# Tap sums of a depthwise convolution kept in PSUM, and two gate blocks ordered behind the last mLSTM head, in a fused RWKV-7, convolution and mLSTM block

## The chip, the core and the metric

One core of a Trainium2 chip runs the whole block as one program. The metric is the device time of one execution in microseconds (us), as the median of several runs. TensorE (PE) multiplies, VectorE (DVE) and ScalarE (ACT) do elementwise work, GpSimd (POOL) does elementwise work beside them, and SyncE's queue (SP) issues all DMAs of this kernel.

## The reference, cut to what matters

```python
def _conv_branch(u, dw, db, ln_w, ln_b, rows):
    a, g = jnp.split(u, 2, axis=-1)
    z = a * jax.nn.sigmoid(g)
    z = _depthwise_conv(z.reshape(B * rows, GRID_W, CONV_W), dw, db)   # 31 taps in rows of 64
    return jax.nn.silu(_layernorm(z, ln_w, ln_b, LN_EPS))
...
def _merge(u_gate, ya, yb, yc, pa, pb, pc, wo):
    ga, gb, gc = jnp.split(jax.nn.sigmoid(u_gate), N_BRANCH, axis=-1)
    m = ga * (ya @ pa) + gb * (yb @ pb) + gc * (yc @ pc)
    return m @ wo
...
# reference(): 512 latent tokens, 256 context tokens, width 1024
h = _rmsnorm(x, g_norm1) * (1 + mod_x[1]) + mod_x[0]
u_rw, u_cv, u_ml, u_gate = jnp.split(h @ w_in, ...)
ya = _rwkv_mixer(...)      # 8 heads, two directions
yc = _mlstm_mixer(...)     # 4 heads of width 128, two directions
yb = _conv_branch(u_cv, ...)                       # 512 channels
x = x + mod_x[2] * _merge(u_gate, ya, yb, yc, ...)
x = x + mod_x[5] * _mlp(h2, w_mlp1, w_mlp2)
return _rmsnorm(x, g_final)
```

`u_gate` is 3072 columns wide: 24 blocks of 128, of which the stage looked at here computes the first six. The convolution's 512 channels are four tiles of 128 channels by 512 tokens.

## The kernel before, in words

Every product with a weight is made in three: a 128x512 half block of weights (`raw`) is loaded by SP, ACT casts it to its high part (`whi`, line 159), POOL subtracts that from `raw` (`wlo`, line 160), and PE multiplies high by high, high by low and low by high (line 293 in this stage). `raw` has three buffers, `whi` and `wlo` four each, so a `wlo` that is late holds back the next load, and the load is a place in SP's queue on which everything behind it waits. `dense(b)` loads block `b` (`wload`) and makes its 24 products of 128x512 for the 512 latent tokens (tile `dl`), and 24 of 128x256 for the context where asked (`dc`). Its PSUM tiles rotate through two banks.

The order of the work: norms and modulation; the features of the RWKV heads, with the first two convolution tiles; the **mLSTM stage** (about 260 to 530 us of the span), with the last two convolution tiles; four pairs of RWKV heads as a recurrent chain (`weave`), with the other 18 gate blocks and the projections beside it; merge and MLP.

In the mLSTM stage `front(h)` makes the four dense blocks of head `h` (`kT`, `vT`, `qT`, `to`), transposes `kT` and `vT`, and builds the states of five chunks for each direction: POOL scales a chunk of keys (`kw`, line 836), PE multiplies it with the values into a PSUM tile `st` (two buffers, line 838), DVE adds it to the running state (`Cst`, lines 840 and 842). `back(h)` makes the scores (`psc`, line 850), the decay masks (`gbc`, `Wd`), per chunk the products `acc` (lines 872 and 873), their normalisation on DVE (lines 875 to 888), four transposes (`pt`, line 889), the gated result `yc` and its store. Traced in this order: `front(0)`, `front(1)`, `back(0)`, the taps of convolution tiles 2 and 3, the preparation of the first RWKV pair (`rw.ctx(0)`, `rw.lat(0)`), `front(2)`, `back(1)`, `front(3)`, `back(2)`, `back(3)`, and six gate blocks `dense(B_GA + g)`, each with a tanh on ACT (line 524) and a store (line 525).

`taps` (line 317) runs over 31 taps of two tiles in turn. Each of its instructions on DVE takes the input tile `z` shifted by one more token, times a weight per channel, plus the sum `y`, into `y` (line 324). Before the change `z` and `y` both lie in SBUF.

Each engine runs its instructions strictly in the order in which the program was built. That order is made by the framework's planner when the program is built: it follows a simulated timeline with costs of its own, takes what is traced first where several instructions are ready, and otherwise fills in later work that is ready. So the taps, the dense blocks and the gate blocks are spread among other work by that plan, not by the chip. `tc.issue_after(ins)` adds to each instruction traced in its block, on the engine of `ins`, that it stands behind `ins` in that engine's order. It makes no semaphore.

Pools share memory as stacks. The RWKV pools opened after the stage lie over what it leaves: the chain's `UV` tiles over the `whi` and `wlo` buffers, its `SV` tiles over `cols`, `kT`, `vT` and the first `qT` buffer, its `xc` and `sps` over both `qT` buffers. The gate results use the tag `qT`. PSUM has eight banks: in this stage two for dense tiles, two for `tp`/`st`, two for `sc` (`psc`, `acc`, `pt`), and on the right side two for the RWKV pool `psa` (tags `g` and `m`).

Of the kernel before, what the change touches and what calls it, by code (L numbers as in the profile page):

```python
# [7 lines left out]
F32 = mybir.dt.float32  # L8
# [6 lines left out]
PSUM = bass.MemoryType.PSUM  # L15
DRAM = bass.MemoryType.DRAM

P = 128
D = 1024
NT = 512  # L20
# [21 lines left out]
B_RW, B_CV, B_ML, B_MG, B_GA = 0, 15, 23, 39, 40  # L42
# [14 lines left out]
NGA = 6  # L57
# [19 lines left out]
def build(tc, wblk, wada, xin, cin, params, lora, consts, rowp, out, dbg=None):  # L77
    nc = tc.nc
    V, A, G, PE, SY = nc.vector, nc.scalar, nc.gpsimd, nc.tensor, nc.sync
# [18 lines left out]
    def CN(name):  # L98
        return cst[:, CO[name]:CO[name] + 128]

    ident = CN("ident")
# [27 lines left out]
    sp = {}  # L129
# [24 lines left out]
    def whalf(b, x, W=None, nr=NRAW, nh=NHI):  # L154
        raw = (W or W0).tile([P, 512], F32, tag="raw", name="raw", bufs=nr)
        SY.dma_start(raw[:, :], wblk[b, :, x * 512:x * 512 + 512])
        hi = (W or W0).tile([P, 512], F32R, tag="hi", name="whi", bufs=nh)
        lo = (W or W0).tile([P, 512], F32R, tag="lo", name="wlo", bufs=nh)
        A.copy(hi[:, :], raw[:, :])  # L159
        G.tensor_tensor(lo[:, :], raw[:, :], hi[:, :], ALU.subtract)  # L160
        return hi, lo

    def wload(b, W=None):
        return [whalf(b, x, W) for x in range(2)]
# [32 lines left out]
    for i in range(4):  # L197
        t = S0.tile([P, D], F32, name=f"xt{i}")
# [3 lines left out]
    for q in range(8):  # L202
        t = S0.tile([P, 4, 512], F32, tag="wada", name="wada", bufs=8)
        SY.dma_start(t[:, :, :], wada[q].rearrange("p (k m) -> p k m", k=4))
        wa.append(t)
        if q == 3:
            for i in range(2):
                t = S0.tile([P, D], F32, name=f"ct{i}")
# [35 lines left out]
    for q in range(4):  # L244
# [5 lines left out]
        pt = PS0.tile([P, 4, 2], F32, tag="pm", name="pm", bufs=1)  # L250
# [27 lines left out]

    PS1 = ed.enter_context(tc.tile_pool(name="ps1", bufs=1, space=PSUM, reuse_waits="tile"))

    def dense(b, lat=True, ctx=False, M=P):
        wts = wload(b)
        res = []
        for seg, use in enumerate((lat, ctx)):
            if not use:
                continue
            ps_ = PSD.tile([P, (NT, NC_)[seg]], F32, tag="d", name=("dl", "dc")[seg], bufs=ND)
            n = 0
            for k in range(KT):
                hi, lo = wts[k // 4]  # L290
                ko = k % 4 * P
                for w, x in ((hi, hh), (hi, hl), (lo, hh)):
                    PE.matmul(ps_[0:M, :], lhsT=w[:, ko:ko + M], rhs=x[seg][:, k, :],  # L293
                              start=(n == 0), stop=(n == 3 * KT - 1))
                    n += 1
            res.append(ps_)
        return res
# [28 lines left out]
    tiles = []  # L326
    for i in range(2):
        z, y = SO.tile([P, 752], F32, name=f"z{i}"), SO.tile([P, NT], F32, name=f"cy{i}")
# [6 lines left out]
    def shifted(b, ctx, name, bufs=1, dst=None):  # L335

        pss = dense(B_RW + b, True, ctx)
        if dst is None:
            dst = S1.tile([P, T if ctx else NT], F32, tag=name, name=name, bufs=bufs)[:, :]
        for ps, a, z in zip(pss, (0, NT), (NT, T)):  # L340
            n = z - a
            A.activation(dst[:, a:z], ps[:, :], AF.Copy, scale=om[:, b:b + 1])
            V.scalar_tensor_tensor(dst[:, a + 1:z], ps[:, 0:n - 1], C("mu_p", b), dst[:, a + 1:z], ALU.mult, ALU.add)
            V.scalar_tensor_tensor(dst[:, a:z - 1], ps[:, 1:n], C("mu_n", b), dst[:, a:z - 1], ALU.mult, ALU.add)
        return dst
# [63 lines left out]
    t = shifted(12, True, "vj", 2)  # L409
    A.activation(wdt[:, :], t, AF.Tanh)  # L410
    t = shifted(13, True, "vj", 2)
# [62 lines left out]
    t = shifted(14, False, "vj", 2)  # L474
# [22 lines left out]
    ec = ExitStack()  # L497
    CZ = ec.enter_context(tc.tile_pool(name="cz", bufs=1, side="right", reuse_waits="tile"))
    SG = eg.enter_context(tc.tile_pool(name="mlg", bufs=1, side="right", reuse_waits="tile"))
    front, back = mlstm(tc, nc, SM, SG, PS1, dense, CN, C, ident, nwh, epsc, sp, sp_rows, dump, consts)  # L500
    eg.close()
    st = [None] * 4
    tiles = [(i, CZ.tile([P, 752], F32, name=f"cz{i}")[:, :], CZ.tile([P, NT], F32, name=f"cy{i}")[:, :]) for i in (2, 3)]
    for i, z, y in tiles:
        SY.dma_start(z, sp["z", i][:, :])
    st[0] = front(0)
# [1 line left out]
    back(0, *st[0])  # L508
    taps(tiles)
    for i, z, y in tiles:  # L510
        SY.dma_start(sp["yb", i][:, :], y)
    ec.close()
    rw = Rwkv(tc, CN, C, ident, epsc, PL, sp, dump)
    rw.open_a()
# [2 lines left out]
    back(1, *st[1])  # L517
    st[3] = front(3)
    back(2, *st[2])
    back(3, *st[3])  # L520
    for g in range(NGA):
        ps, = dense(B_GA + g)
        t = SM.tile([P, NT], F32, tag="qT", name="gt", bufs=2)
        A.activation(t[:, :], ps[:, :], AF.Tanh, scale=0.5)
        SY.dma_start(sp["g", g][:, :], t[:, :])
# [27 lines left out]
    acc = {}  # L553
# [165 lines left out]
def mlstm(tc, nc, S, SG, PS1, dense, CN, C, ident, nwh, epsc, sp, sp_rows, dump, consts):  # L719
    V, A, G, PE, SY = nc.vector, nc.scalar, nc.gpsimd, nc.tensor, nc.sync  # L720
# [21 lines left out]
    b = SG.tile([R, T], F32, name="b")  # L742
# [8 lines left out]
    g = t1.rearrange("p (c t) -> p c t", c=6)  # L751
# [27 lines left out]
    for c2 in range(2):  # L779
        pt = PS1.tile([P, 3, 3, R], F32, tag="tp", name="tp", bufs=2)  # L780
        for ci in range(3):
            c = c2 * 3 + ci
# [64 lines left out]
    def back(h, qT, kT, to, v1, qs, Cst):  # L847
        psc = PS1.tile([P, NT], F32, tag="sc", name="psc", bufs=2)
        for c in range(4):
            PE.matmul(psc[:, c * 128:(c + 1) * 128], lhsT=kT[:, c * 128:(c + 1) * 128], rhs=qT[:, c * 128:(c + 1) * 128],  # L850
                      start=True, stop=True)
        Wd = []
        for d in range(2):
            rr = rows[d] + h
            gbc = S.tile([P, NT], F32, tag="gbc", name="gbc", bufs=2)
            SY.dma_start(gbc[:, :], sp_rows[d][h:h + 1, 0:NT].partition_broadcast(P))
            nm = nms[:, d * 128:d * 128 + 128]
            for c in range(4):
                V.scalar_tensor_tensor(gbc[:, c * 128:(c + 1) * 128], gbc[:, c * 128:(c + 1) * 128],
                                       cols[:, c, 0, rr:rr + 1], nm, ALU.add, ALU.add)  # L860
            A.activation(gbc[:, :], gbc[:, :], AF.Exp)
            wd = S.tile([P, NT], F32, tag="Wd", name="Wd", bufs=2)
            V.tensor_tensor(wd[:, :], psc[:, :], gbc[:, :], ALU.mult)
            Wd.append(wd)
        ht = S.tile([P, 4, 128], F32, tag="ht", name="ht")
        stats = S.tile([P, 4, 6], F32, tag="stats", name="stats")
        mv = S.tile([P, 4, 2], F32, tag="mv", name="mv")
        for c in range(4):
            acc = PS1.tile([P, 2, 129], F32, tag="sc", name="acc", bufs=2)
            for d in range(2):  # L870
                p = orders[d].index(c)
                PE.matmul(acc[:, d, :], lhsT=Wd[d][:, c * 128:(c + 1) * 128], rhs=v1[:, c, :], start=True, stop=False)
                PE.matmul(acc[:, d, :], lhsT=qs[d][:, c * 128:(c + 1) * 128], rhs=Cst[d][:, p - 1, :], start=False, stop=True)
            dn = S.tile([P, 2], F32, tag="dn", name="dn", bufs=2)
            V.scalar_tensor_tensor(dn[:, :].unsqueeze(2), acc[:, :, 128:129], -1.0, cols[:, c, 1, h:h + 33:32].unsqueeze(2),
                                   ALU.mult, ALU.max)
            V.tensor_tensor(dn[:, :].unsqueeze(2), dn[:, :].unsqueeze(2), acc[:, :, 128:129], ALU.max)
            V.reciprocal(dn[:, :], dn[:, :])
            V.tensor_scalar(ht[:, c, :], acc[:, 0, 0:128], dn[:, 0:1], None, ALU.mult)
            V.scalar_tensor_tensor(ht[:, c, :], acc[:, 1, 0:128], dn[:, 1:2], ht[:, c, :], ALU.mult, ALU.add)  # L880
            V.bn_stats(stats[:, c, :], ht[:, c, :])
            V.bn_aggr(mv[:, c, :], stats[:, c, :])
        var = S.tile([P, 4], F32, tag="var", name="var")
        V.tensor_scalar(var[:, :].unsqueeze(2), mv[:, :, 1:2], 1e-5, None, ALU.add)
        rstd = rsqrt(nc, S, var[:, :], 4)
        pt = PS1.tile([P, NT], F32, tag="sc", name="pt", bufs=2)
        for c in range(4):
            V.tensor_scalar(ht[:, c, :], ht[:, c, :], mv[:, c, 0:1], rstd[:, c:c + 1], ALU.subtract, ALU.mult)
            PE.transpose(pt[:, c * 128:(c + 1) * 128], ht[:, c, :], ident)
        yc = S.tile([P, NT], F32, tag="yc", name="yc")  # L890
        V.scalar_tensor_tensor(yc[:, :], pt[:, :], nwh[:, h:h + 1], to[:, :], ALU.mult, ALU.mult)
        SY.dma_start(sp["yc", h][:, :], yc[:, :])

    return front, back

# [626 lines left out]
```

## Time and profile before

| what | value |
|---|---|
| median of three runs | 1374.11 us (1370.31 to 1378.94) |
| the profiled execution, its own time | 1368.34 us |
| its span, first to last instruction | 1366.6 us |
| mean granted TensorE clock | 0.955 |
| PE busy | 1238.3 us (91%) |
| DVE busy | 858.2 us (63%) |
| POOL busy | 583.0 us (43%) |
| ACT busy | 511.2 us (37%) |

All times of instructions below are those of the one profiled execution, in us from the span's start unless marked ns. The medians are of other executions of the same program. A granted clock of 1.00 is TensorE's upper level of 2.4 GHz. Busy shares are of the whole span.

### The profile page before, as it was taken

To read this page: it belongs to the slowest core of one execution; us is meant where nothing else is said; L and a number is where in the kernel's file an instruction comes from. 1 tells how busy PE (TensorE), PEld (TensorE's weight loads), DVE (VectorE), ACT (ScalarE), POOL (GpSimd) and SP (SyncE) were. 2 spreads that over 40 slices of the span, in tenths; PEclk is the share of its full clock that TensorE was granted. 3 is DMA by queue.
4 is the path that set the end of the run, shared out by engine and by line. 5 is a ranking of instruction groups with operands and counts; after the bars stand their busy time and mean duration, and the time that the engine had idled before them with its cause. 6 is when DMAs were issued, how large, how long until landed. Compare 5 with 4: busy or idle time off the path is not lost.

```text
span 1366.6 us, 21733 instructions
## 1 busy us (share of the span) xinstructions
PE 1238.3 (91%) x8020; PEld 964.7 (71%) x8020; DVE 858.2 (63%) x1513; ACT 511.2 (37%) x1048; POOL 583.0 (43%) x547
## 2 busy tenths in 40 slices
PE   5989989776999886998998888989999999999997
PEld 2678867565888675666676555667887878888886
DVE  5698788798357984796978957688284533300202
ACT  4426567432222221342443445322364333322222
POOL 1633434329554523332433454433465544444542
PEclk9999999888999998998999998999999999999999
DMA  9312688722622315241431254876444422432332
GB/s 375 99 58 63 197 264 245 229 75 70 200 78 91 125 53 150 85 131 60 136 117 48 86 164 146 275 247 234 139 131 142 136 93 93 154 101 95 129 98 87
DMA packets 101457, 187.85 MB, mean 137 GB/s; under 512 B 10708, under 2 KB 29396, under 8 KB 100328
## 3 DMA queue, kind: packets, MB, share of 16 engines
q1 hardware_dynamic: 101352, 186.47, 43.0%
q8 instruction: 63, 1.03, 0.3%
q14 instruction: 42, 0.34, 0.1%
HBM read 148.64 MB, written 29.40 MB: 130 GB/s over the span
## 4 chain that ended last, share of the span: by engine, by line
PE 42%; DVE 17%; DMA 6%; issue 2%; ACT 1%; POOL 0%; SPq 0%; DVEq 0%; ACTq 0%; POOLq 0%
PE pt L1301 16%; PE pd L1370 13%; DMA wad<-wada 5%; PE dg L545 4%; DVE N L1052 3%; DVE tmp L1050 3%; PE pg L1006 2%; DVE N L1045 2%; DVE accm L641 1%; PE pd L715 1%; DVE LT L1075 1%; PE ch L1133 1%; DVE SV L1149 1%; PE dl L293 1%; PE ch L1139 1%
## 5 line engine op out<-in xcount | busy, mean ns | idle before, releaser
L160 POOL TENSOR_TENSOR wlo<-raw,whi 128x512 fp32r<-128x512 f32 x296 | 430.8, 1461 | 554.8 <-ACT whi L159 496.3
L159 ACT CAST whi<-raw 128x512 fp32r<-128x512 f32 x296 | 181.7, 619 | 322.0 <-PE pt L1301 114.1
L293 PE MATMUL dl<-hh,whi 128*128 128x512 f32 (+1 forms) x344 | 143.2, 416 | 5.2 <-ACT kT L791 4.3
L293 PE MATMUL dl<-hh,wlo 128*128 128x512 f32 (+1 forms) x344 | 140.5, 408 | 0.0
L293 PE MATMUL dl<-hl,whi 128*128 128x512 f32 (+1 forms) x344 | 139.7, 406 | 0.0
L1370 PE MATMUL pd<-h2h,wlo 128*128 128x512 f32 (+1 forms) x272 | 105.2, 388 | 0.0
L1370 PE MATMUL pd<-h2l,whi 128*128 128x512 f32 (+1 forms) x272 | 104.5, 386 | 0.6 <-POOL h2l L1353 0.6
L1396 DVE TENSOR_TENSOR x<-pt,modb 128x512 f32<-128x512 f32 x8 | 5.5, 691 | 154.8 <-PE pt L1301 154.8
L1370 PE MATMUL pd<-h2h,whi 128*128 128x512 f32 (+1 forms) x272 | 102.3, 383 | 0.2 <-ACT h2h L1350 0.2
L1301 PE MATMUL pt<-whi,h1l 128*128 128x512 f32 x256 | 99.7, 389 | 0.0
L1301 PE MATMUL pt<-whi,h1h 128*128 128x512 f32 x256 | 99.7, 389 | 0.0
L1301 PE MATMUL pt<-wlo,h1h 128*128 128x512 f32 x256 | 99.2, 389 | 0.0
L293 PEld LDWEIGHTS dl<-hh,whi 128*128 128x128 f32 (+1 forms) x344 | 66.9, 194 | 20.4 <-ACT kT L791 4.5
L1374 DVE TENSOR_TENSOR relu<-relu 128x512 f32<-128x512 f32 x32 | 43.7, 1367 | 57.9 <-ACT relu L1373 57.8
L641 DVE SCALAR_TENSOR_TENSOR accm<-wad,scz,accm 128x512 f32<-128x512 f32 x56 | 57.6, 1028 | 34.2 <-DMA wad<-wada 33.6
L293 PEld LDWEIGHTS dl<-hh,wlo 128*128 128x128 f32 (+1 forms) x344 | 66.8, 194 | 14.3 <-issue 0.4
L293 PEld LDWEIGHTS dl<-hl,whi 128*128 128x128 f32 (+1 forms) x344 | 66.6, 194 | 13.8 <-issue 1.3
L1146 POOL TENSOR_TENSOR sps<-SV,PL 64x128 f32<-64x128 f32 x88 | 40.0, 454 | 78.6 <-DVE SV L1149 75.5
L545 PE MATMUL dg<-hl,whi 128*128 128x512 f32 x144 | 65.8, 457 | 0.0
L545 PE MATMUL dg<-hh,whi 128*128 128x512 f32 x144 | 65.0, 451 | 0.0
L545 PE MATMUL dg<-hh,wlo 128*128 128x512 f32 x144 | 64.9, 450 | 0.0
L1370 PEld LDWEIGHTS pd<-h2l,whi 128*128 128x128 f32 x272 | 51.7, 190 | 12.5 <-POOL h2l L1353 0.9
(399 smaller groups left out, 2824.7 us busy)
## 6 DMA issues: line engine op xcount, KB each, us to landing
raw<-wblk SPq DMA_DIRECT2D x296, 256.0 KB, 2.9
wad<-wada SPq DMA_DIRECT2D x64, 256.0 KB, 4.1
wada<-wada SPq DMA_DIRECT2D x8, 1024.0 KB, 12.0
BK<-kb SPq DMA_DIRECT2D x16, 384.0 KB, 5.1
sp_bk<-BK SPq DMA_DIRECT2D x8, 768.0 KB, 5.5
BK<-sp_bk SPq DMA_DIRECT2D x8, 768.0 KB, 4.2
sp_g<-gt SPq DMA_DIRECT2D x24, 256.0 KB, 2.0
sp_al<-al SPq DMA_DIRECT2D x8, 640.0 KB, 5.2
```

The lines of the kernel that those rows point to most:

```text
L159: A.copy(hi[:, :], raw[:, :])
L160: G.tensor_tensor(lo[:, :], raw[:, :], hi[:, :], ALU.subtract)
L293: PE.matmul(ps_[0:M, :], lhsT=w[:, ko:ko + M], rhs=x[seg][:, k, :], start=(n == 0), stop=(n == 3 * KT - 1))
L545: yield lambda w=w, x=x, k=k, ko=ko, n=n: PE.matmul(ps[:, :], lhsT=w[:, ko:ko + P], rhs=x[:, k, :], start=(n == 0), stop=(n == 3 * KT - 1))
L641: V.scalar_tensor_tensor(o, t[:, :], sc[:, k, 0:1], o, ALU.mult, ALU.add)
L1006: PE.matmul(ps[hf, i, :, :], lhsT=BK[dd, c, x, :], rhs=al[:, c] if lat else AL[d][dd, 8 + c:9 + c, :], start=True, stop=True)
L1050: V.tensor_tensor(tv, N[:, s + 1:32, s:s + 1].to_broadcast([P, n, s]), N[:, s:s + 1, 0:s].to_broadcast([P, n, s]), ALU.mult)
L1052: V.tensor_tensor(N[:, s + 1:32, 0:s], N[:, s + 1:32, 0:s], tv, ALU.add)
L1146: last["Pool"] = G.tensor_tensor(sps[hf], SV[d][hf, c, :, :], PL[hf, c, :].unsqueeze(2).to_broadcast([64, 2, CH]), ALU.mult)
L1301: PE.matmul(pss[i][:, :], lhsT=x[:, k, ts_], rhs=w[:, :], start=(k == 0 and n == 0), stop=(k == nk - 1 and n == 2))
L1370: PE.matmul(ps[:, ts_], lhsT=w[:, ko:ko + P], rhs=x[:, k, ts_], start=(k == 0 and n == 0), stop=(k == 7 and n == 2))
L1374: V.tensor_tensor(t[:, :], t[:, :], t[:, :], ALU.mult)
```

## The change

The running sums `y` of convolution tiles 2 and 3 get a PSUM pool of their own (two banks on the right side); after the last tap ACT copies each to an SBUF tile, which is stored as before. The pool is closed ahead of the RWKV pools, so `psa` lies on the same two banks. `dense` can be handed weights that are loaded already. `back` returns two instructions, the last product of `acc` and the last transpose. Gate blocks 0 to 3 are made as before; the weights of blocks 4 and 5 are loaded as before, but the 24 products of block 4 stand behind head 3's last `acc` product in PE's order, and those of block 5 behind its last transpose.

```diff
-    def dense(b, lat=True, ctx=False, M=P):
-        wts = wload(b)
+    def dense(b, lat=True, ctx=False, M=P, wts=None):
+        wts = wts or wload(b)
...
-    tiles = [(i, CZ.tile([P, 752], F32, name=f"cz{i}")[:, :], CZ.tile([P, NT], F32, name=f"cy{i}")[:, :]) for i in (2, 3)]
+
+    CP = ec.enter_context(tc.tile_pool(name="cp", bufs=1, space=PSUM, side="right", reuse_waits="tile"))
+    tiles = [(i, CZ.tile([P, 752], F32, name=f"cz{i}")[:, :], CP.tile([P, NT], F32, name=f"cy{i}")[:, :]) for i in (2, 3)]
...
     taps(tiles)
     for i, z, y in tiles:
-        SY.dma_start(sp["yb", i][:, :], y)
+        t = CZ.tile([P, NT], F32, name=f"ct{i}")
+        A.copy(t[:, :], y)
+        SY.dma_start(sp["yb", i][:, :], t[:, :])
     ec.close()
...
-    back(3, *st[3])
+    marks = back(3, *st[3])
     for g in range(NGA):
-        ps, = dense(B_GA + g)
+
+        if g < NGA - 2:
+            ps, = dense(B_GA + g)
+        else:
+            wts = wload(B_GA + g)
+            with tc.issue_after(marks[g - NGA + 2].ins):
+                ps, = dense(B_GA + g, wts=wts)
...
-                PE.matmul(acc[:, d, :], lhsT=qs[d][:, c * 128:(c + 1) * 128], rhs=Cst[d][:, p - 1, :], start=False, stop=True)
+                last = PE.matmul(acc[:, d, :], lhsT=qs[d][:, c * 128:(c + 1) * 128], rhs=Cst[d][:, p - 1, :], start=False, stop=True)
...
-            PE.transpose(pt[:, c * 128:(c + 1) * 128], ht[:, c, :], ident)
+            end = PE.transpose(pt[:, c * 128:(c + 1) * 128], ht[:, c, :], ident)
...
+        return last, end
```

## Rows read from the trace of the kernel before

**Rows 1.** Busy time by stretch: start:end, length, PE, PEld, DVE, ACT, POOL, granted clock, DMA.
```profile
327.00:339.00 12.00, 1.20 (x8) 0.77 (x7) 7.32 (x12) 0.80 (x2) 12.00 (x5) 0.76 0.13 43
339.00:344.00 5.00, 5.00 (x16) 4.13 (x17) 3.24 (x5) 0.10 (x1) 5.00 (x6) 0.56 0.38 131
344.00:440.00 96.00, 94.35 (x676) 80.46 (x675) 51.03 (x161) 24.64 (x46) 50.39 (x57) 0.98 0.41 121
```

**Rows 2.** PE in order of time, 317 to 350 us: start, length, instruction.
```profile
327.57 0.40 PE L293 MATMUL dl<-hl,whi 128*128 128x512 f32 x1
...
338.77 0.80 PE L838 MATMUL st<-v,kw 128*128 128x129 f32 x2 [10.80 <-POOL kw L836]
...
339.79 0.63 PE L293 MATMUL dl<-hh,whi 128*128 128x512 f32 x1
...
346.98 0.38 PE L838 MATMUL st<-v,kw 128*128 128x129 f32 x2
```

**Rows 3.** POOL in order of time, 317 to 352 us.
```profile
321.25 15.40 POOL L160 TENSOR_TENSOR wlo<-raw,whi 128x512 fp32r<-128x512 f32 x2 [3.38 <-ACT whi L159]
```

**Rows 4.** DVE in order of time, 317 to 352 us.
```profile
319.66 14.65 DVE L324 SCALAR_TENSOR_TENSOR cy<-cz,dwh,cy 128x512 f32<-128x512 f32 x22
339.61 0.29 DVE L840 COPY Cst<-st 128x129 f32<-128x129 f32 x1 [5.29 <-PE st L838]
```

**Rows 5.** Views of single lines: count, then shortest, median and longest in ns.
```profile
L324 DVE SCALAR_TENSOR_TENSOR cy<-cz,dwh,cy x60: 734/743/1779, 268.3 to 343.2; 128x512 f32<-128x512 f32 x60
...
L160 POOL TENSOR_TENSOR wlo<-raw,whi x12: 1254/1740/14185, 272.8 to 340.5; 128x512 fp32r<-128x512 f32 x12
...
L343 DVE SCALAR_TENSOR_TENSOR vj<-dl,par,vj x11: 737/745/751, 77.7 to 259.6; 128x511 f32<-128x511 f32 x11
...
L1017 DVE TENSOR_TENSOR AL<-pg,cst x48: 416/683/695, 364.6 to 736.8; 64x512 f32<-64x512 f32 x32, 64x256 f32<-64x256 f32 x16
...
L485 ACT COPY gtt<-tp x4: 561/585/587, 270.0 to 288.9; 128x512 f32<-128x512 f32 x4
...
L1006 PE MATMUL pg<-AL,BK x768: 217/269/473, 362.7 to 735.7; 64*64 64x128 f32 x127, 64*64 64x64 f32 x65
```

**Rows 6.** PE's waits from 262 to 346 us: total, times, longest.
```profile
PE dl L293 <- ACT kT L791: 4.3, 1, 4.3
```

**Rows 7.** PE in order of time, 498 to 537 us.
```profile
511.01 0.38 PE L872 MATMUL acc<-v,Wd 128*128 128x129 f32 x2
...
517.39 0.39 PE L293 MATMUL dl<-hl,whi 128*128 128x512 f32 x1
517.62 0.40 PE L293 MATMUL dl<-hh,wlo 128*128 128x512 f32 x1
...
519.41 0.39 PE L873 MATMUL acc<-Cst,qs 128*128 128x129 f32 x2
525.98 1.16 PE L889 MATMUL pt<-cst,ht 128*128 128x128 f32 x4 [6.18 <-DVE ht L888]
531.34 1.35 PE L1133 MATMUL ch<-SV,AL 128*64 128x64 f32 x8 [4.21 <-DMA SV<-sp_v]
```

**Rows 8.** DVE in order of time, 440 to 545 us.
```profile
505.54 1.29 DVE L863 TENSOR_TENSOR Wd<-psc,gbc 128x512 f32<-128x512 f32 x2 [0.96 <-PE psc L850]
...
514.39 0.23 DVE L875 SCALAR_TENSOR_TENSOR dn<-acc,cols 128x2 f32<-128x2 f32 x2 [3.30 <-PE acc L873]
...
518.95 0.16 DVE L875 SCALAR_TENSOR_TENSOR dn<-acc,cols 128x2 f32<-128x2 f32 x1 [2.23 <-PE acc L873]
...
524.20 1.25 DVE L73 SCALAR_TENSOR_TENSOR rsq<-rsqt,rsq 128x4 f32<-128x4 f32 x1
```

**Rows 9.** SP's queue in order of time, 440 to 545 us.
```profile
528.37 1.29 SPq L1100 DMA_DIRECT2D SV<-sp_v  x2
529.72 1.28 SPq L1100 DMA_DIRECT2D UV<-sp_v  x2
```

**Rows 10.** The page, part 6: DMA issues, size, median us from issue to landing.
```profile
sp_g<-gt SPq DMA_DIRECT2D x24, 256.0 KB, 2.0
```

## The prediction, made before the changed kernel had run

> **What bounds the kernel now.** I read the busy shares first: PE is busy for 91% of the span, every other engine for under two thirds, so PE's order sets the end and a gain has to be time in which PE stands still or runs at the lower clock. The second view is busy time by stretch over the mLSTM stage, where both edits lie. From 344 to 440 PE is busy for 94.35 of 96.00 us [rows 1]: what PE loses ahead of that stretch is not made good in it, and nothing in the kernel waits for a fixed moment, so it is lost at the end too. The third view is PE in order of time, looked through for idle time and for what ended it. Around the two edits it shows three holes: 10.80 us ahead of 338.77, ended by POOL's `kw` [rows 2]; 6.18 us ahead of head 3's transposes, ended by DVE; and 4.21 us ahead of the RWKV chain's first product, ended by the load of `SV` [rows 7].
>
> **The hole at 328 to 339 us.** PE's dense product starts at 327.57, and the next instruction, `st`, starts at 338.77 [rows 2]. POOL's `kw` stood behind two `wlo` that took 15.40 us together from 321.25 [rows 3], one of them 14185 ns, where the shortest took 1254 ns [rows 5]. In the same time DVE ran 22 taps without a gap, 319.66 to 334.31 [rows 4]; the two `wlo` ended at 336.65. The long one therefore ended about 1.1 us after the burst (336.65 less a short one, 1.25, is 335.40), nearly the whole of a short `wlo` again. It did next to nothing until the burst was over. The reverse shows too: the taps, median 743 ns, reach 1779 ns, while an instruction of the same kind that reads one operand from PSUM, line 343, stays between 737 and 751 ns over 11 instances [rows 5]. So two SBUF operands on DVE and a subtraction on POOL hinder each other, and one operand in PSUM takes DVE out of it.
>
> The Trainium skill has a rule for this: its page "SBUF — State Buffer", section "Who interferes with whom", says that a DVE instruction with two SBUF inputs contends with a GpSimd instruction that reads SBUF, and that with at most one SBUF input it does not. The trace agrees with the pairing, by the 14185 against the 1254 ns. The page also has the loser blocked until the instruction that holds the port finishes; that bound does not fit the long one, which lasted through 22 of them.
>
> What the first edit gives here, with the order kept:
> - The hole, 10.80 us, goes.
> - Behind it PE ran from 339 to 344 at a granted clock of 0.56, near the lower level (1.2 of 2.4 GHz), after those idle microseconds: nine dense products at 0.63 us instead of the 0.40 just before the hole [rows 1, 2], 9 x 0.23 = 2.1 us. It goes with the hole.
> - What is late next: `st` has two buffers, so the third `st` needs `Cst` of the first, and that stands on DVE behind the 22 taps (it ran at 339.61, but DVE was through with the burst at 334.31 [rows 4]). Between the first `st` and the third (346.98 [rows 2]) PE has 20 dense products at the 0.23 from one to the next of full speed (517.39 to 517.62, [rows 7]), 4 half as wide and one `st`, about 5.3 us; without the hole the third is due at 327.9 + 5.3 = 333.2, and `Cst` is done at 334.31 + 0.29 = 334.6. That is 1.4 us of new wait, and 0.7 for the next one, which has one more tap ahead of it: +2.1.
> - Elsewhere in the stage: PE waited once 4.3 us for ACT's `kT` [rows 6], in a chain that goes back to DVE's work among contended taps. I take 1.0 of it, bounds 0 and 4.3.
>
> **What a tap costs in PSUM.** No row shows DVE writing PSUM. Below, the nearest row is line 1017, with a PSUM operand and 512 elements: 683 ns, 0.06 less than a tap. Line 343, which is the same operation with a pointer scalar and a PSUM operand, has 745 ns, as a tap now. Above, if reading and writing the same bank took turns, a second pass over 512 elements: line 1017 takes 416 ns for 256 elements and 683 for 512, so 0.53 us more per tap. I take 745 ns, the same operation, and so no change of DVE's length; 57 of the 60 taps lie ahead of `Cst`, so the lower end is -3.4 us and the upper +30, which is a rival below. The skill's page "Perfetto Trace Analysis", section "Optimizing Scalar/DVE Operations", speaks against the edit: about 125 ns of access for DVE on PSUM against 60 on SBUF. By that the 57 taps would take an estimated 3.7 us longer, and the time come out at 1363 instead of the 1359 below; line 343 against the taps shows no such difference.
>
> **What the first edit adds.** Two ACT copies of 585 ns (line 485, [rows 5]), on an engine busy for 24.64 of 96 us there [rows 1]. They add a wait: ACT's queue stands until the last tap, where SP's stood for the store before, and behind it are the casts `whi` and the evictions of `vT`. The last taps run between `Cst` steps, about where PE ends the latent half of `vT`; the 24 short context products behind it, some 2.9 us, cover a wait of up to that. I take +0.3, and up to 2 if the copies stand just ahead of the eviction. The stores lie where they lay. `psa` now needs the copies' banks, but its first writer starts at 362.7 (line 1006, [rows 5]), 18 us after the last tap: nothing, as long as the preparation of the RWKV pair stays that far behind. Sum of the first edit: -10.8 - 2.1 + 2.1 - 1.0 + 0.3 = -11.5 us.
>
> **The second edit.** Of the 48 products of gate blocks 4 and 5, 41 stand between head 3's scores and its last `acc` [the last at 517.62, rows 7]. Moved behind, they let head 3 go. `Wd` is done at 506.83 [rows 8]; the `acc` products of two chunks, eight instructions at the pitch of a dense one, take 1.9 us, so DVE's first normalisation can start at 508.8 instead of 514.39, 5.6 earlier. From there to the transposes it took 11.59 us, of which 2.23 were a wait for the second pair of `acc` [rows 8] that PE's dense work had put off, and one `rsq` on 128x4 elements took 1.25 us where a `dn` on half of that takes 0.16 [rows 8]. So the transposes could come 5.6 + 2.2 + 1.1 = 8.9 us earlier. Against it: PE then has more idle time before block 4, and at the lower clock the block's 24 products take some 10 us instead of 24 x 0.23 = 5.5, which can put the transposes off, to a bound of 3 earlier. I take 6.5.
>
> After the transposes the chain began 4.2 us later (531.34 against 527.14). Now block 5 stands there, 5.5 us. The `UV` tiles lie over the weight buffers that block 5 reads, so their load can go only behind it and blocks SP for what follows; before, it went 2.6 us after the transposes [rows 9]. That is 3 us later. If `SV` itself has to wait for the store of the last gate tile, it is 5.5 + 0.6 of tanh + 0.1 + 2.0 of store [rows 10] + 3.0 of load = 11.2 against 4.2, 7 us later. I take 3, since the last tile used the second `qT` buffer before and `SV` lies over the first. Waiting on it is the whole chain, and behind that load SP's loads of the next weights. The weights of both blocks are loaded when they were and only hold their four buffers longer; the next weights go to another pool's buffers, so that costs nothing. Sum: -6.5 + 3.0 = -3.5, bounds -8 and +4.
>
> **Sum.** -11.5 - 3.5 = -15 us: 1368.3 becomes 1353.3 for an execution like the profiled one, whose span is 1366.6 with 1.7 around it. The profiled execution is 5.8 below the median of the runs, so I put the forecast at 1374.1 - 15 = 1359 us.
>
> **Rivals.**
> - *DVE takes the place of POOL.* With POOL free, the burst of taps still stands ahead of `Cst`, and the planner, which works with its own costs of a PSUM operand, lays a new order with another long burst or a copy ahead of an eviction. For it: DVE ran without a gap through that burst. Against it: only 2.1 us by the present order. It would keep 5 to 8 us in all: about 1367.
> - *The gates hold the chain back.* The bound of +4 in place of -3.5, with the first edit as summed: 1366.5. For it: SP's order is fixed, and the store is the only thing in front of `SV` that moves later.
> - *The edit doesn't unblock POOL.* If a tap could hold a `wlo` up only for its own length, that one would have taken 1.25 + 0.74 = 2.0 us, the hole would have another cause (POOL's spans are rough), and only the second edit would count: 1370. Against it stand the burst's end and the reverse effect on the taps. That bound is the one that the Trainium skill's page on SBUF states, in the section named above.
> - *Slower: a tap in place takes two passes.* 57 taps of 0.53 us more put `Cst` to about 364; PE then waits from 333 to 364, 31 us against the 12.9 of now, and the RWKV preparation moves behind it. With the second edit's -3.5 that is +15 and more: about 1390. It decides from a tap of about 0.93 us, where 57 x 0.2 us eat the first edit's gain. For it only that no row shows such an instruction; against it that operations reading PSUM run at the length of the others.
>
> **How the numbers follow.** Forecast 0.58, own range 1350 to 1365; DVE or planner 0.16; gates 0.10; POOL not unblocked 0.07; two passes 0.09. A measurement of this kernel can tell about 1% from no change, 13.7 us: faster means under 1360.4. The forecast lies just under that line; some 0.46 of its 0.58 I put under it and 0.12 above, and with a little from a planner's order that is luckier than mine, 0.48 for faster. Slower by over 1% is the two passes and a little from a bad order: 0.10. The rest, 0.42, is within. The range leaves out the two passes and as much at the lower end: 1346 to 1375.
>
> **What would show it.** In the changed profile: the longest `wlo` between 262 and 346 under 2.5 us and no PE hole of over 4 us ended by `kw`; taps at 680 to 760 ns with none over 1000; PE at 1.00 where it was 0.56; block 4 between `acc` and the transposes, block 5 between the transposes and the chain; `SV` issued ahead of the last gate store. The prediction is wrong if taps take 0.9 us and more, if a PE wait for `Cst` or `vT` of over 5 us stands in the old hole's place, or if the chain's first product waits more than 4 us for its load.

## The result and the profile after

The changed kernel takes 1353.68 us (median of 6 runs, 1352.62 to 1362.72) against 1372.38 for the kernel before beside it: ratio 0.9871, 95% interval 0.9833 to 0.9910. The profiled execution took 1353.13 us with a span of 1351.3; that of before had 1366.6, so the spans differ by 15.3 us.

Line numbers are up to 11 higher than before: `kw` is 846, `st` 848, `Cst` 850 and 852, `acc` 882 and 883, `pt` 899, the chain's first product 1144, its loads 1111. Busy time by stretch, changed kernel, in the stretches of [rows 1] and two more (columns as there):

```profile
327.00:339.00 12.00, 12.00 (x70) 10.48 (x69) 11.80 (x21) 2.72 (x5) 6.46 (x9) 1.00 0.28 85
339.00:344.00 5.00, 5.00 (x26) 4.13 (x25) 2.96 (x6) 2.55 (x5) 3.88 (x5) 1.00 0.47 148
...
262.00:346.00 84.00, 75.73 (x389) 62.38 (x389) 66.51 (x103) 28.89 (x48) 34.35 (x33) 0.93 0.33 106
...
440.00:517.40 77.40, 58.57 (x451) 49.47 (x449) 59.11 (x169) 16.89 (x32) 25.08 (x27) 0.84 0.23 78
```

The hole is gone: PE is busy for all of 327 to 344 at a granted clock of 1.00, where 0.56 stood from 339 to 344. The last row is the stretch ahead of the chain: 18.8 us of idle PE, at 0.84. The same for the kernel before, in the stretches that the next paragraphs use:

```profile
262.00:346.00 84.00, 66.13 (x308) 52.56 (x307) 70.50 (x98) 22.74 (x38) 42.35 (x22) 0.86 0.30 101
...
440.00:531.30 91.30, 71.66 (x536) 59.92 (x535) 73.60 (x195) 22.11 (x42) 34.85 (x36) 0.91 0.30 95
```

Idle time of PE from 262 to 346 falls from 17.87 to 8.27 us; ahead of the chain it is 19.64 before and 18.83 after, with the clock at 0.91 before and 0.84 after (0.92 in a second profile of the changed kernel, `e13_changed`). Nearly all the gain in idle time is in the first stretch. What POOL and DVE do there, changed kernel, single lines (count, then shortest, median and longest in ns):

```profile
L160 POOL TENSOR_TENSOR wlo<-raw,whi x17: 1268/1296/2258, 271.2 to 344.3; 128x512 fp32r<-128x512 f32 x17
L324 DVE SCALAR_TENSOR_TENSOR cy<-cz,dwh,cy x60: 739/744/755, 295.1 to 341.1; 128x512 f32<-128x512 f32 x60
```

The same two engines there in order of time:

```profile
309.16 1.30 POOL L160 TENSOR_TENSOR wlo<-raw,whi 128x512 fp32r<-128x512 f32 x1 [2.58 <-ACT whi L159]
...
308.10 18.52 DVE L324 SCALAR_TENSOR_TENSOR cy<-cz,dwh,cy 128x512 f32<-128x512 f32 x28
326.53 0.28 DVE L850 COPY Cst<-st 128x129 f32<-128x129 f32 x1
```

And PE's waits in that stretch:

```profile
PE tp L794 <- DVE ri L764: 7.6, 1, 7.6
```

A burst of 28 taps runs without a gap, and the subtractions beside it take 1.30 us, where one took 14185 ns [rows 5]; the longest of the stretch is 2258 ns. A tap takes 744 ns; its longest went from 1779 [rows 5] to 755. One wait is new: 7.6 us for `ri`, of the gate rows. The taps now start at 290.60, behind the scans of those rows; before, they stood between them from 267.7.

The end of the stage in order of time, changed kernel, PE, SP's queue and POOL, to be read against [rows 7, 9]:

```profile
501.09 0.39 PE L883 MATMUL acc<-Cst,qs 128*128 128x129 f32 x2
...
506.80 0.79 PE L899 MATMUL pt<-cst,ht 128*128 128x128 f32 x4
...
517.42 1.05 PE L1144 MATMUL ch<-SV,AL 128*64 128x64 f32 x8 [4.36 <-POOL SV L1114]
...
513.73 0.33 SPq L535 DMA_DIRECT2D sp_g<-gt  x1
514.16 1.31 SPq L1111 DMA_DIRECT2D SV<-sp_v  x2
...
514.29 2.48 POOL L160 TENSOR_TENSOR wlo<-raw,whi 128x512 fp32r<-128x512 f32 x2 [24.44 <-ACT whi L159]
516.71 0.52 POOL L926 MEMSET LT<- 128x512 f32 x1
517.17 0.45 POOL L1114 MEMSET SV<- 64x128 f32 x2
```

Block 4 fills 501.24 to 506.80 and block 5 507.34 to 513: the transposes wait for nothing. But in SP's order the load of `SV` stands behind the store of the last gate tile, 5.3 us after that of the last `yc` (508.40), and the chain starts 10.6 us after the transposes, where it was 5.4 [rows 7].

### The profile page after: what moved, and what is told of

It reads as the page before. It is cut to its first block, busy times and chain, and to the rows that moved or that the text cites. A ratio compares the mean times of both kernels' runs of the same rounds, so it can differ in the third digit from the quotient of the medians.

```text
span 1351.3 us, 21724 instructions
## 1 busy us (share of the span) xinstructions
PE 1236.0 (91%) x8020; PEld 963.8 (71%) x8020; DVE 845.7 (63%) x1513; ACT 512.2 (38%) x1050; POOL 564.5 (42%) x547
## 4 chain that ended last, share of the span: by engine, by line
PE 54%; DVE 17%; DMA 7%; issue 3%; ACT 2%; POOL 1%; SPq 1%; DVEq 0%; POOLq 0%; ACTq 0%
PE pt L1312 16%; PE pd L1381 13%; PE dl L293 5%; DMA wad<-wada 5%; PE dg L555 5%; DVE N L1063 4%; PE pg L1017 3%; DVE tmp L1061 2%; PE dc L293 2%; PE pd L725 1%; PE ch L1144 1%; DVE N L1056 1%; DVE accm L651 1%; PE pbk L1042 1%; PE ch L1150 1%
## 5 line engine op out<-in xcount | busy, mean ns | idle before, releaser
L160 POOL TENSOR_TENSOR wlo<-raw,whi 128x512 fp32r<-128x512 f32 x296 | 413.8, 1402 | 562.5 <-ACT whi L159 509.6
L651 DVE SCALAR_TENSOR_TENSOR accm<-wad,scz,accm 128x512 f32<-128x512 f32 x56 | 53.5, 956 | 38.1 <-DMA wad<-wada 37.6
L1063 DVE TENSOR_TENSOR N<-N,tmp 128x30 f32<-128x30 f32 (+14 forms) x120 | 61.1, 509 | 2.9
```

The source lines that it names most:

```text
L651: V.scalar_tensor_tensor(o, t[:, :], sc[:, k, 0:1], o, ALU.mult, ALU.add)
L1063: V.tensor_tensor(N[:, s + 1:32, 0:s], N[:, s + 1:32, 0:s], tv, ALU.add)
```

## The experiments

**Each edit alone.** Theory: an accumulator in SBUF holds POOL up, and POOL holds PE up. Rivals: the gate blocks carry the gain; or only the taps' later start does (the next experiment).

```diff
 # e1_taps: the first edit; the gate loop as before
 # e2_gates: the second edit; the taps' tiles from CZ as before
```

> First edit alone: the 62 taps of tiles 2 and 3 add up in PSUM with the two copies behind them; all six gate blocks are issued as in the kernel before. Theory (the accumulator in SBUF holds POOL up, and POOL holds PE up): most of the gain is here, 11.5 us of the sum of 15, ratio to before about 0.9915; wlo between 262 and 346 us under 2.5 us each, no PE wait for kw over 4 us. Rival (the second edit carries the gain): ratio 0.997 to 1.000. The changed kernel measured 0.987.

> Second edit alone: gate block 4 behind the last head's last accumulator product and block 5 behind its last transpose; the taps add up in SBUF as before. Theory: worth about 3.5 us (ratio 0.9975), the 10.8 us hole of PE before kw stays. Rival (this edit carries the gain): ratio 0.990 or less. Second rival (the blocks hold the recurrence's chain back): ratio 1.000 or more, the chain's first product not earlier than in the kernel before (531.3 us).

The first edit alone: 0.9866 (0.9803 to 0.9929). The second alone: 0.9978 (0.9939 to 1.0017). Together they gave 0.9871, so in the times the first carries it all and the second adds nothing that can be told from zero. With the second alone the hole stays: PE waits 9.5 us for `kw`. PE and SP at the end of the stage, first edit alone:

```profile
505.57 0.39 PE L877 MATMUL acc<-Cst,qs 128*128 128x129 f32 x2
512.02 1.15 PE L893 MATMUL pt<-cst,ht 128*128 128x128 f32 x4 [6.06 <-DVE ht L892]
517.36 1.14 PE L1138 MATMUL ch<-SV,AL 128*64 128x64 f32 x8 [4.18 <-DMA SV<-sp_v]
...
513.99 0.33 SPq L896 DMA_DIRECT2D sp_yc<-yc  x1
514.41 1.30 SPq L1105 DMA_DIRECT2D SV<-sp_v  x2
```

And second edit alone:

```profile
520.77 0.79 PE L895 MATMUL pt<-cst,ht 128*128 128x128 f32 x4
531.42 0.74 PE L1140 MATMUL ch<-SV,AL 128*64 128x64 f32 x8 [4.36 <-POOL SV L1110]
...
527.72 0.33 SPq L531 DMA_DIRECT2D sp_g<-gt  x1
528.15 1.31 SPq L1107 DMA_DIRECT2D SV<-sp_v  x2
```

The chain starts at 517.42 and 517.36 with the first edit, and at 531.42 and 531.34 [rows 7] without. These starts can't be compared as they stand, because each profile is of one execution: the changed kernel profiled twice (`e13_changed`, below) has the chain at 517.42 and at 522.81. What can be compared is the length of the stage. In all of these profiles PE has made the same 1129 products when the last `bo` starts on DVE (line 455, the end of the stage before, which no edit of this table touches), and makes 1506 or 1507 from there to the chain:

| kernel | last `bo` | chain | between | PE idle | PE busy | clock |
|---|---|---|---|---|---|---|
| before | 263.61 | 531.34 | 267.7 | 39.2 | 228.5 | 0.92 |
| second edit (`e2_gates`) | 262.64 | 531.42 | 268.8 | 38.1 | 230.7 | 0.92 |
| both edits | 261.56 | 517.42 | 255.9 | 28.1 | 227.8 | 0.93 |
| both edits again (`e13_changed`) | 265.01 | 522.81 | 257.8 | 32.7 | 225.1 | 0.95 |
| first edit (`e1_taps`) | 264.79 | 517.36 | 252.6 | 29.2 | 223.4 | 0.95 |
| one block held (`e7_one_block`, below) | 263.43 | 511.77 | 248.3 | 23.7 | 224.7 | 0.94 |

The two profiles of one kernel are 1.9 us apart, so a difference of that size says nothing. The first edit takes 15.2 us off the stage. The second alone changes it by +1.1, which can't be told from nothing; beside the first it makes the stage 3.3 and 5.2 us longer.

The second edit does bring the transposes close behind the last `acc` product: 5.7 us after it with the blocks held, 6.5 with the first edit alone, without a wait. But the chain then starts 10.6 us behind the transposes (10.65 with the second edit alone) in place of 5.3 and 5.4. And ahead of the transposes other waits come back, as if the held products had covered them. PE's wait for `Cst`, both edits and then the first alone:

```profile
487.65 1.20 PE L848 MATMUL st<-v,kw 128*128 128x129 f32 x4 [5.31 <-DVE Cst L852]
...
490.94 0.46 PE L842 MATMUL st<-v,kw 128*128 128x129 f32 x2 [2.00 <-DVE Cst L846]
```

All such waits of `st` together are 4.6 to 6.7 us in the five profiles of this case with two blocks held, 0.2 to 3.0 in the three with one, and 0.2 to 2.0 in the four with none. The load of `SV` stands behind another store in SP's order: `yc`'s at 513.99, or the last gate's at 513.73.

**The place of the accumulator against the taps' start.**

```diff
 # e4_sbuf_same, in taps(): s is one more tile of CZ
-    z, y = (...)(z, y)
+    z, y, o = (...)(z, y if k == 1 else s, y if k in (0, 30) else s)
-    V.scalar_tensor_tensor(y, z[...], w, y, ...)
+    V.scalar_tensor_tensor(o, z[...], w, y, ...)
```

> The first edit alone, but only the first and the last tap of each tile write PSUM; the 58 taps between them read and write an accumulator in SBUF. The PSUM tiles, the two copies and the stores stay, so that the taps stay behind the gate rows' scans, where the changed kernel has them (290 us and not 268 us). Theory (the accumulator's place in SBUF stretches POOL's subtractions): wlo of 5 us and more come back between 295 and 341 us, PE waits again for kw, and the gain of the first edit is lost, ratio to before 0.997 to 1.004. Rival (the later start of the taps, behind the scans, is what helps): wlo may stretch, but the ratio is that of the first edit alone, within 0.003.

0.9997 (0.9964 to 1.0030). This kernel is the first edit with 58 of the 62 taps on an accumulator in SBUF. DVE, POOL and PE in order of time show:

```profile
309.85 18.63 DVE L324 SCALAR_TENSOR_TENSOR cs<-cz,dwh,cs 128x512 f32<-128x512 f32 x28
...
310.92 19.91 POOL L160 TENSOR_TENSOR wlo<-raw,whi 128x512 fp32r<-128x512 f32 x2 [3.38 <-ACT whi L159]
...
329.65 0.79 PE L293 MATMUL dl<-hh,wlo 128*128 128x512 f32 x1 [12.30 <-POOL wlo L160]
```

The same burst of 28 at the same place, but one of the two subtractions takes 18678 ns (a view of line 160), and PE waits 12.30 us for it. The 7.6 us for `ri` stand in this kernel too: they belong to the later start, and not to the place of the sum. The fourth corner, PSUM early:

```diff
 # e10_early: e1_taps, and for the products from gdt
-    pl = PS1.tile([P, NT], F32, tag="tp", name="tp", bufs=1)
+    pl = PS1.tile([P, NT], F32, tag="st", name="tp", bufs=2)
```

> The first edit alone, with one further line: the last products of the stage before (tile tp from gdt) take the two places of the low-rank products in PSUM, so that the bank that the second accumulator takes is free earlier. On DVE the first taps then stand ahead of the scans of the gate rows, as in the kernel before, and not behind them. With the run in SBUF at the late place this gives the fourth corner: SBUF early 1.000, SBUF late 1.000, PSUM late 0.987 measured. Theory (the place of the accumulator decides, not the taps' start): ratio 0.982 to 0.990, no subtraction over 3 us between 262 and 346 us. Rival (the late start was a part of the gain): 0.992 or more.

0.9863 (0.9832 to 0.9893); `wlo` there, and the first taps, which now stand ahead of the scans:

```profile
L160 POOL TENSOR_TENSOR wlo<-raw,whi x17: 1272/1292/2578, 274.9 to 344.5; 128x512 fp32r<-128x512 f32 x17
...
280.89 1.53 DVE L322 TENSOR_SCALAR cy<-cz,dwh,par 128x512 f32<-128x512 f32 x2 [3.37 <-ACT gtt L485]
```

So the four corners are 1.000 and 0.9997 with SBUF, 0.9863 and 0.9866 with PSUM: the place decides, and the start makes no difference that can be told. That the taps waited for the bank under `tp` is shown by the same line: with that bank free earlier they moved ahead.

**Which operand, and at what price.**

```diff
 # e5_bench, e6_bench: nothing but phases like this one
+    for k in range(20):
+        V.scalar_tensor_tensor(dst, z[:, :, k:k + 64], w[k], src, mult, add)
+        if k < 12: G.tensor_tensor(wlo, raw, whi, subtract)
```

> Not the kernel's computation: phases of 20 taps of 128x512 on DVE and 12 subtractions raw - whi of 128x512 on POOL, each alone and side by side, twice over; the accumulator in SBUF, in PSUM, read from SBUF and written to PSUM, read from PSUM and written to SBUF, and in the last phase a DVE operation with one input only. Theory: a subtraction takes about 1.3 us alone and beside taps whose accumulator is in PSUM, and several us beside taps that read two operands from SBUF; a tap takes about 735 ns in SBUF and 745 ns in PSUM. If the written side decides, the phase that reads SBUF and writes PSUM is free of the stretch; if the read side decides, the phase that reads PSUM and writes SBUF is. Rival (POOL's stretch has another cause in the kernel, as its inputs' place or its queue): all phases show the same subtraction.

Its phases ran into one another (a tap on the SBUF accumulator between two on the PSUM one), so it doesn't tell the operands apart. The mended one:

> Not the kernel's computation: the phases of taps and subtractions of the first such run, which ran into one another there, now each behind the end of the one before. Theory: 12 subtractions take about 15.5 us (1.3 us each) alone and beside taps with the accumulator in PSUM; beside taps that read two operands from SBUF some are held for the length of the tap burst, as the 18.7 us one beside the SBUF accumulator in the second half of the convolution. If the read side decides, the phase that reads SBUF twice and writes PSUM is held up, and the phase that reads PSUM and writes SBUF is free; if the written side decides, the other way round. Rival (the cause lies elsewhere in the kernel): all phases alike at about 15.5 us.

Its lines by phase, first the taps (alone in SBUF, alone in PSUM, then beside POOL: SBUF; PSUM; SBUF read and PSUM written; PSUM read and SBUF written; the form with one input), then POOL's subtractions alone and beside the third to the sixth:

```profile
L113 DVE SCALAR_TENSOR_TENSOR ysb<-z,par,ysb x20: 752/752/752, 23.3 to 38.3; 128x512 f32<-128x512 f32 x20
L113 DVE SCALAR_TENSOR_TENSOR yps<-z,par,yps x20: 756/756/756, 39.4 to 54.5; 128x512 f32<-128x512 f32 x20
L113 DVE SCALAR_TENSOR_TENSOR ysb<-z,par,ysb x20: 751/1631/1665, 55.6 to 81.4; 128x512 f32<-128x512 f32 x20
L113 DVE SCALAR_TENSOR_TENSOR yps<-z,par,yps x20: 755/756/756, 82.6 to 97.6; 128x512 f32<-128x512 f32 x20
L113 DVE SCALAR_TENSOR_TENSOR yps<-z,par,ysb x20: 758/1631/1662, 99.4 to 125.1; 128x512 f32<-128x512 f32 x20
L113 DVE SCALAR_TENSOR_TENSOR ysb<-z,par,yps x20: 747/748/748, 126.4 to 141.2; 128x512 f32<-128x512 f32 x20
L118 DVE TENSOR_SCALAR ysb<-z,par x20: 485/1366/1402, 143.1 to 163.7; 128x512 f32<-128x512 f32 x20
...
L108 POOL TENSOR_TENSOR wlo<-raw,whi x12: 1261/1262/1262, 6.9 to 21.6; 128x512 fp32r<-128x512 f32 x12
L108 POOL TENSOR_TENSOR wlo<-raw,whi x12: 1588/1614/1762, 55.8 to 74.4; 128x512 fp32r<-128x512 f32 x12
L108 POOL TENSOR_TENSOR wlo<-raw,whi x12: 1260/1288/1297, 82.7 to 97.7; 128x512 fp32r<-128x512 f32 x12
L108 POOL TENSOR_TENSOR wlo<-raw,whi x12: 1587/1603/1761, 99.5 to 118.1; 128x512 fp32r<-128x512 f32 x12
L108 POOL TENSOR_TENSOR wlo<-raw,whi x12: 1266/1278/1287, 126.5 to 141.4; 128x512 fp32r<-128x512 f32 x12
```

The read side decides: with two inputs from SBUF a tap goes from 752 to 1631 ns whichever memory it writes, and with one from PSUM it stays at 748 to 756; POOL's subtractions go the same way, 1603 to 1614 against 1278 to 1288. A PSUM accumulator costs 4 ns a tap. That half of the expectation held; the other, that subtractions are held for the length of the burst, did not show here: each takes 1.61 us, about as long as a tap beside it.

**One block held in place of two.**

```diff
 # e7_one_block
-        if g < NGA - 2:
+        if g < NGA - 1:
-            with tc.issue_after(marks[g - NGA + 2].ins):
+            with tc.issue_after(marks[0].ins):
```

> The changed kernel, but gate block 4 is free again and block 5 alone is behind the last head's last accumulator product. With the first edit alone the chain's first product came at 517.4 us, 3.0 us after the SV load, which waited for the last yc store; in the changed kernel it also came at 517.4 us, 3.3 us after an SV load that waited for the last gate store. Theory (the held blocks only change what the SV load waits for, and give up work that covered other waits): one block fits the 6.1 us wait before the transposes and is over when they start, so the chain starts about 5 us earlier, ratio about 0.983. Rival (the chain's start is set by the sum of PE's work and the order gives nothing): ratio as the changed kernel, 0.986 to 0.988.

0.9847 (0.9801 to 0.9893), median 1349.59, span 1343.6. PE and SP:

```profile
499.35 0.39 PE L883 MATMUL acc<-Cst,qs 128*128 128x129 f32 x2
...
505.03 0.80 PE L899 MATMUL pt<-cst,ht 128*128 128x128 f32 x4
511.77 1.14 PE L1144 MATMUL ch<-SV,AL 128*64 128x64 f32 x8 [5.94 <-DMA SV<-sp_v]
...
506.65 0.33 SPq L902 DMA_DIRECT2D sp_yc<-yc  x1
...
508.14 1.31 SPq L1111 DMA_DIRECT2D SV<-sp_v  x2
```

The block fits between the last `acc` and the transposes, neither of the two stores is late, and PE's wait for `Cst` is 0.5 us. The interval of the ratio alone leaves room for the rival. The stage speaks against it: 248.3 us, where the changed kernel took 255.9 and 257.8 and the first edit alone 252.6. With the earlier taps of `e10_early` as well, and the changed kernel once more on the same chip:

> Both single steps together: block 5 alone held behind the last accumulator product, and the last products of the stage before in the low-rank products' places. Theory: the two lie in different stretches and add up; if the early start is worth nothing, ratio as block 5 alone, 0.982 to 0.987.

> The changed kernel once more, on the chip of the three runs beside it, so that they can be read against it: 0.984 to 0.990. Theory (of the two held blocks, one gives work up that covered other waits): slower than the kernel with block 5 alone held, by 2 to 6 us.

0.9836 (0.9788 to 0.9885) and 0.9878 (0.9836 to 0.9919). By these ratios the kernels with one block held are 0.2 and 0.4% under the changed one, 3 and 6 us, with intervals that overlap; that the time of the whole falls is therefore likely and not shown. The earlier taps add nothing that can be told: the stage takes 248.4 us with them, from 262.32 to 510.72.

**The first half's taps.**

```diff
 # e8_all_taps: tiles 0 and 1 from PSUM, with copies; tags n and st with bufs=1
 # e9_fewer_banks: tags n and st with bufs=1, taps as they were
 # e11_one_tile: e7_one_block, tile 0 from PSUM, tag n with bufs=1
```

> The changed kernel with the first half's taps (tiles 0 and 1) in PSUM as well, with two copies; two banks are freed for them by giving two buffers of that stage (the low-rank products' and the normalisation's) one place in place of two. Theory: the 60 taps there that took 54.2 us (939 ns mean) fall to about 745 ns, 11.6 us less of DVE, and the subtractions in the first 262 us fall from 1683 to about 1400 ns; what that is worth is bounded by PE's waits of that stretch for DVE and POOL, about 10 us without the start: ratio to before 0.980 to 0.987. Rival (the chain of that stage is set elsewhere, or the missing buffers cost as much): 0.987 or more.

> The changed kernel with the two freed buffers alone, the first half's taps in SBUF: the price of the room in the run with all taps in PSUM. Theory: at most 2 us, ratio 0.987 to 0.989. If the single buffers cost more, the run with all taps in PSUM is to be read against this one.

> The kernel with block 5 alone held, and tile 0 of the first half's taps in PSUM beside tile 1 in SBUF, in one bank that the normalisation's second buffer gives up; the low-rank products keep both of theirs, whose loss delayed the operands of the recurrence by some 15 us in the runs with two banks freed. Theory: half of what all taps in PSUM gave against their control (0.6%), so 3 to 4 us less than block 5 alone: ratio 0.980 to 0.984. Rival (the single buffer costs as much, or alternating taps already let POOL through): 0.984 to 0.990.

`e8_all_taps` 0.9936 (0.9905 to 0.9967), `e9_fewer_banks` 0.9995 (0.9959 to 1.0032), `e11_one_tile` 0.9865 (0.9827 to 0.9902). The taps did what was expected: 748 ns median there, 756 at most, and 0.6% against the run with the two buffers gone (the two intervals just overlap). But the two buffers cost 1.2%, far over the 2 us expected: with them gone PE waits, between 262 and 346 us, 9.3 us for `lf`, 8.9 for the evictions of the low-rank products, whose buffer was made single, and 6.2 for `gtt`; the changed kernel has none of the three there. The planner also laid a new order, with the first `ri` at 293.32 us in place of 269.13, so how much each lost buffer costs by itself is not shown. One tile in PSUM for one buffer gains nothing over `e7_one_block`. In that stage the two banks are worth more as second buffers than to the taps.

## Why the prediction was right, step by step

**The sum was right, its two parts were not, and that it fits so well is luck.** By the spans of the profiled executions it is -15 summed against -15.3. But 2.05 us of these were won ahead of the stage, where the kernels make the same products and two profiles of the changed kernel differ by 3.45 (261.56 and 265.01), and 1.4 behind the chain's start. In the stage itself it is -11.9, and -9.9 by the second profile. The medians fell by 18.7 us, 1372.38 to 1353.68, with an interval of 12.4 to 22.9 (by that of the ratio) that holds -15 as well. By part, the first edit alone takes 15.2 us off the stage where 11.5 were summed, and the second adds 3.3 and 5.2 beside it where -3.5 stood. The errors have opposite signs and partly cancel.

**First edit.** The mechanism was right: the hole of 10.80 went, and so did the rival of an edit that doesn't unblock POOL, since `e4_sbuf_same` brings a subtraction of 18678 ns back and loses all. The term for `kT` was mis-sized: of the 4.3 us wait [rows 6] I took 1.0, and all of it went. The wait for `Cst` (+2.1) did not come: I kept the order, but in the changed kernel the burst starts 11.6 us earlier than in [rows 4] (9.5 counted from the last `bo`), and `Cst` runs right behind it at 326.53, ahead of PE's need. In its place came what I had not summed, a longer wait for `ri`, 7.8 us in the run with the first edit alone against 1.2, from the planner's new order. In that run PE's idle time in the stage falls by 10.0 us (39.2 to 29.2), near the 15.1 of the two waits that went less the 6.6 that `ri` adds; and its busy time by 5.2 (228.5 to 223.4) for the same products, at a clock of 0.95 against 0.92: the term of 2.1 for the clock was too small as well. The ACT copies took 1.07 us together and no PE wait stands behind them.

**The tap's price.** 745 ns taken, 744 measured, so the rival of two passes is out. The Trainium skill's page "Perfetto Trace Analysis", section "Optimizing Scalar/DVE Operations", would have made the taps longer; 752 against 756 ns in one kernel show next to none of that.

**Second edit.** The step that failed is the start of the chain: "3 us later" against the transposes, with `SV` issued ahead of the last gate store and with next weights that cost nothing. `SV` is issued behind that store in both kernels that hold the blocks (513.73 and 514.16; 527.72 and 528.15), and the chain came 5.2 us later against the transposes (10.6 against 5.4). Nor did the transposes come 6.5 us earlier: counted from the last `bo` it is 4.2 with the second edit alone, and 2.0 and 0.1 beside the first, with the waits that came back ahead of them. That is the rival of the gates that hold the chain back; its price in the sum was +4, and beside the first edit the stage shows +3.3 and +5.2. PE's last wait, 4.36 us, is also over the 4 us that I had named as a sign of being wrong, though it is not for the load. It ends with POOL's fill of `SV`, which begins at 517.17, behind `wlo` of the next block, which waited 24.4 us for `whi`, and that stands on ACT behind the last tanh. The loads of `SV` take 2.8 us to land, so by an estimate from its issue at 514.16 the first was there at 517.0. Both ways thus end within 0.4 us of each other, and an earlier load alone would have gained next to nothing; neither was moved by itself.

## What to carry to other kernels

When one engine's short instructions last ten times their shortest, look at what runs beside them on the engine that reads the same memory: moving one operand of the neighbour to PSUM cost 4 ns a tap and took 15 us off the stage. Holding work back to fill a later wait pays only up to the length of that wait and while nothing behind it becomes the last; count the store of the held work and what is queued behind that, and try one piece less. Compare two profiles from an event ahead of the change: one kernel's two profiles had the chain's start 5.4 us apart, 3.45 of them from before the stage. A saving with a price in buffers needs a control run with the price alone.

## What the runs showed that I had not expected

Whether POOL is slowed or shut out seems to go by the gaps between DVE's instructions. In `e6_bench`, where each tap waits for the one before on the same accumulator, 20 taps alone take 15.71 us (785 ns apart, 752 each), and beside POOL both go on at 1.6 us each. In the kernel, taps alternate between two accumulators and follow at 18.63 / 28 = 0.67 us, less than the 0.74 that one takes: the next begins before the last ends, and one subtraction stood through the burst, 18678 ns in `e4_sbuf_same`. No run changed the spacing alone, so this stays a reading of two cases.

The Trainium skill's page "SBUF — State Buffer", section "Who interferes with whom", has the pairs right: two SBUF inputs contend and one does not, as the phases of `e6_bench` show. It has the loser wait for one instruction; by the 18678 ns, at 0.67 us a tap, it was more than 25 of them in that burst.

One form with a single SBUF input contends all the same: the `TENSOR_SCALAR` from SBUF to SBUF takes 485 ns at its shortest and a median of 1366 beside POOL. The same section names that operation among those that can, in its two-port mode; the subtractions beside it, 12 in 17.09 us against 16.00 alone, lose little.
